# Attention with eight query heads on two key heads: the linear step of an exponential made on VectorE in place of GpSimd, groups of eight in place of ten, K placed from GpSimd's queue

## The chip, the cores and the metric

The kernel runs on one core of a Trainium2 chip. The metric is the time of one execution in microseconds of the device. Three executions of the kernel before gave 389.97, 390.28 and 391.14 us; the median is 390.28.

The core has engines that run beside one another: TensorE (PE, matmuls; PEld is its loading of weights), VectorE (DVE), ScalarE (ACT), GpSimd (POOL) and SyncE (SP), which issues DMAs. Each works through its own queue in order and waits on semaphores of others. ScalarE and GpSimd can issue DMAs too.

## The reference

Inputs are q of 8 x 8 x 1024 x 64 (batch, query heads, positions, head width), k and v of 8 x 2 x 1024 x 64, all fp32 and about 0.1 in size. Four query heads share one key head.

```python
scale = 1.0 / np.sqrt(head_dim)
for g in range(n_kv_heads):
    scores = scale * np.matmul(q_group, k_group.transpose(0, 1, 3, 2))
    scores_max = np.max(scores, axis=-1, keepdims=True)
    attn = np.exp(scores - scores_max)
    attn = attn / (np.sum(attn, axis=-1, keepdims=True) + 1e-08)
    output[:, q_start:q_end, :, :] = np.matmul(attn, v_group)
```

The kernel doesn't subtract the maximum, since the scores are small. It gets each row's sum from a column of ones beside v.

## The kernel before

**Jobs and cells.** A job is one batch, one query head and one of two sides (the even or the odd query positions, 512 of them): 128 jobs in all. Each job has eight cells, one for each 128 key positions. A cell is one score matmul (line 426), an exponential of its 128 x 512 scores, and four output matmuls (line 490) that add up in one bank for the job. There are 1024 cells.

**Two ways to the exponential.** A cell of kind A goes to ScalarE, two cells at a time: one ACTIVATE of 128 x 1024 (line 437, tile pa). A cell of kind D goes to VectorE. Line 446 (planner's name p1) turns its scores into the bits of a bf16 number, by one multiplication and addition written as uint16. That is a rough exponential. When GROUP of these cells are gathered in a tile pd, a chain of four steps corrects all of them at once: step 0 (line 462) takes the fraction bits into z; step 1 (line 468) makes y, a linear function of z, in fp16; step 2 (line 478) multiplies y by z; step 3 (line 482) adds y to pd. The steps named in POOL_STEPS run on GpSimd, the others on VectorE. Before, step 1 is on GpSimd and GROUP is 10.

**The end of a job.** VectorE takes the reciprocal of the sums (line 503) and multiplies the outputs by it (line 506); SP stores the result (line 515).

**The planner.** The order of all this is written out ahead of time by make_plan. It simulates the engines with fixed prices (QK, PV, P1, NORM, EXP, and CHAIN as a constant and a part per cell for each of the four steps) and always takes the operation that can start first, with ties by kind. Kind A takes the cells of the current job; kind D takes cells of jobs that lie LEAD ahead (fewer at the start: one job for every RAMP jobs done), at most PER_JOB of one job, while fewer than PENDING cells wait for the end of their chain and fewer than LIVE_D groups are alive. So the prices and these limits decide how many cells go each way. A plan step that is on GpSimd is taken not to occupy VectorE.

**Loads.** A head of q or k is cast to bf16 by a DMA of GpSimd's queue into scratch memory (line 299), where it waits for a recent score matmul, so that casts keep pace with the work. SP's queue then turns it with two transposing DMAs (line 311) into qT or kT. K is held zero-padded in kset: for each side the 64 rows of one half of the partitions are zero. Four DMAs for each batch and key head (place_k, line 319) copy the pieces of kT there: 60 in all, since the first is made by other means. Values are loaded by GpSimd's queue (place_v, line 332). All of these have due times counted back from the first use of their head, th: for late heads a k cast at th - 36.5, its transposes at th - 26, the placements at th - 15, the v loads at th - 12, a q cast at th - 27 and its transposes at th - 18. at_pool is at, except that it moves a due time that falls in a GpSimd chain step to the end of that step. Each queue gets its steps in order of due time.

Of the kernel before, what the change touches and what calls it, by code (L numbers as in the profile page):

```python
# [11 lines left out]

CURVE_A, CURVE_B = 0.32988085, -0.33401025

GROUP = 10
POOL_STEPS = (1,)


def make_plan(nj, nkc):
# [6 lines left out]

    QK, PV, P1, NORM = 0.216, 0.1225, 0.603, 0.555
    EXP = (0.065, 0.4265)
    CHAIN = ((0.20, 0.133), (0.25, 0.43), (0.16, 0.27), (0.16, 0.27))
    FROM_PE, FROM_ACT, FROM_DVE, FROM_POOL = 0.26, 0.17, 0.10, 0.15  # L30
    LIVE_A, LIVE_D, PENDING, PER_JOB, LEAD, RAMP, AHEAD, FIRST_PV = 28, 5, 20, 2, 8, 6, 0.08, 2.0
    INF = 1e9
    FIRST_LOAD, EACH_LOAD = 4.5, 4.2
    ops = []
# [20 lines left out]
    while normed < nj:  # L55
# [22 lines left out]
        for i, s in enumerate(open_jobs):  # L78
            for c in rem[s]:
                at = max(pe, FIRST_PV, ready.get(s * nkc + c, INF))  # L80
                if at < INF:
                    best = min(best or (INF,), (at, 3 + i, "pv", (s, c)))
        if len(open_jobs) < 2 and next_job < nj:
            at = min(ready.get(next_job * nkc + c, INF) for c in range(nkc))
            at = max(pe, FIRST_PV, min(obank_free), at)
            if at < INF:
                best = min(best or (INF,), (at, 3 + len(open_jobs), "open", next_job))
        for q, p, kind in ((normq, 0, "norm"), (p1q, 1, "p1"), (chainq, 2, "chain")):
            if q:
                at = q[0][0]  # L90
                if kind != "chain" or q[0][3] not in POOL_STEPS:
                    at = max(dve, at)
# [64 lines left out]
        elif kind == "p1":  # L157
# [8 lines left out]
            home[cell] = ("D", d_id)  # L166
            if len(cur) == GROUP:
                chainq.append((dve + FROM_DVE * (0 in POOL_STEPS), d_id, cur, 0))
                cur = []
        elif kind == "flush":  # L170
            chainq.append((dve + FROM_DVE * (0 in POOL_STEPS), d_id, cur, 0))
            cur = []
        else:
            _, g, cells, step = chainq.pop(0)
            ops.append((t, "chain", g, len(cells), step))
            end = t + CHAIN[step][0] + CHAIN[step][1] * len(cells)
            dve = end if step not in POOL_STEPS else dve
            if step + 1 < len(CHAIN):
                at = end
                if (step in POOL_STEPS) != (step + 1 in POOL_STEPS):  # L180
                    at += FROM_POOL if step in POOL_STEPS else FROM_DVE
                chainq.insert(0, (at, g, cells, step + 1))
# [9 lines left out]
def kernel(  # L192
# [7 lines left out]
    nc = tc.nc  # L200
# [30 lines left out]

    jobs = [(b, h, side) for b in range(B) for h in range(H) for side in range(2)]
    plan = make_plan(len(jobs), NKC)
    starts = {}
    for op in plan:
# [44 lines left out]
    def at(t, f, *args):  # L280
        events.append((t, len(events), f, args))

    def at_pool(t, f, *args):

        for first, last in chains:
            if first - POOL_DMA < t < last:
                t = last + 0.01
        at(t, f, *args)
# [27 lines left out]
        transpose(("k", b, g), kT[(b, g)], n)  # L316

    def place_k(b, g, side, parity):
        nc.sync.dma_start(  # L319
            out=ksets[b % 2][  # L320
                side * D : (side + 1) * D, g, side, parity * HALF : (parity + 1) * HALF
            ],
            in_=kT[(b, g)][parity * D : (parity + 1) * D, :],
        )
# [118 lines left out]
    def exp_bits(cell, n, g, slot):  # L443
        if slot == 0:
            groups[g] = pd_pool.tile([128, GROUP, QBS], U16, name="pd")
        nc.vector.tensor_scalar(  # L446
# [9 lines left out]
    def exp_curve(g, m, step):  # L456
        pd = groups[g][:, 0:m]
        eng = nc.gpsimd if step in POOL_STEPS else nc.vector
        if step == 0:
            z = tmp_pool.tile([128, GROUP, QBS], U16, name="z")[:, 0:m]  # L460
            temps[g] = [z]
# [3 lines left out]
        elif step == 1:  # L465
            y = tmp_pool.tile([128, GROUP, QBS], FP16, name="y")[:, 0:m]
            temps[g].append(y)
# [55 lines left out]
    for op in plan:  # L523
        if op[1] == "qk":
            first_use.setdefault(op[2] // (2 * NKC), op[0])
        elif op[1] == "norm":
            b, h, side = jobs[op[2]]
# [10 lines left out]
    for b in range(B):  # L538
        for h in range(H):
            if b == 0 and h == 0:  # L540
                continue
            th = first_use[b * H + h]
            spare = min(1.0, max(0.0, th - 12.0) / 60.0)
            if (b, h) not in ((0, 1), (0, 2)):
                casts.append((th - 13.0 - 14.0 * spare, ("q", b, h), q[b, h]))
            for n in range(HALF // PIECE):
                at(th - 8.0 - 10.0 * spare + n, transpose_q, b, h, n)
            if h % HPG == 0:
                g = h // HPG
                th = min(first_use[b * H + h + i] for i in range(HPG))  # L550
                casts.append((th - 16.5 - 20.0 * spare, ("k", b, g), k[b, g]))
                for n in range(HALF // PIECE):
                    at(th - 11.0 - 15.0 * spare + n, transpose_k, b, g, n)
                for side in range(2):
                    for parity in range(2):
                        at(th - 6.0 - 9.0 * spare, place_k, b, g, side, parity)
                for two in range(2):
                    at_pool(th - 4.0 - 8.0 * spare + two, place_v, b, g, two)
    casts.sort(key=lambda e: e[0])
# [43 lines left out]
```

## Time and profile before

| what | us |
|---|---|
| median of three runs | 390.28 |
| the profiled execution, whole | 391.14 |
| its span, first to last instruction | 389.4 |
| ScalarE busy | 376.5, of them 374.0 in 406 exponentials |
| TensorE busy | 362.7 |
| VectorE busy | 350.6 |
| GpSimd busy | 166.6, of them 94.6 in 22 chain steps |
| DMA, mean rate | 117 GB/s |

The granted TensorE clock is 1.000 in the whole span. Busy times are unions: an instruction that starts while the one before it drains adds only what it adds. So the mean duration of an ACTIVATE is 1060 ns, but 406 of them fill 374.0 us, 921 ns each. In a row of groups the parts are: line, engine, operation, tiles and shapes, count, then busy time and mean nanoseconds of one, then the engine's idle time before these instructions and what ended most of it.

### The profile page before, as it was taken

The numbers are of one execution on the slowest core, as the hardware profiler recorded it, in microseconds if no ns is written. First come the engines' busy times: TensorE is split into PE (matmuls) and PEld (weight loads), VectorE is DVE, ScalarE is ACT, GpSimd is POOL, SyncE is SP. The second block draws the span as 40 slices with busy tenths as digits, with TensorE's granted clock in tenths as the row PEclk, the third lists the DMA queues.
The fourth block names the chain that finished last, engine by engine and source line by source line (L and its number), as shares of the span: only waits on it lengthen the run. The fifth ranks groups of instructions, "written<-read, shape, count | busy, mean of one in ns | idle before, by whom it ended". The sixth has DMA issues, their size and how long they took to land.

```text
span 389.4 us, 12414 instructions
## 1 busy us (share of the span) xinstructions
PE 362.7 (93%) x5080; PEld 234.1 (60%) x5172; DVE 350.6 (90%) x545; ACT 376.5 (97%) x410; POOL 166.6 (43%) x147
## 2 busy tenths in 40 slices
PE   7979999989999998999999999999999999999986
PEld 5425565556566665676666656666555666665654
DVE  4789999889989999899999999999998999999782
ACT  5999999989999999999999999999999999999995
POOL 5494543437152543525254463525165352421410
PEclk9999999999999999999999999999999999999999
DMA  7768949494958676595968658493775948220213
GB/s 128 130 136 108 139 89 135 105 162 95 152 103 123 140 126 124 110 155 108 157 130 129 141 101 136 109 185 83 131 133 106 165 103 135 67 73 29 65 47 82
DMA packets 104921, 45.52 MB, mean 117 GB/s; under 512 B 66272, under 2 KB 103393, under 8 KB 103617
## 3 DMA queue, kind: packets, MB, share of 16 engines
q1 hardware_dynamic: 84592, 31.22, 34.2%
q0 software_dynamic: 19728, 13.25, 30.4%
q8 instruction: 40, 0.66, 0.7%
q10 hardware_dynamic: 544, 0.26, 0.2%
q14 instruction: 17, 0.13, 0.2%
HBM read 25.17 MB, written 27.00 MB: 134 GB/s over the span
## 4 chain that ended last, share of the span: by engine, by line
ACT 66%; PE 16%; issue 6%; DMA 5%; DVE 5%; SPq 2%; POOL 0%; POOLq 0%; ACTq 0%
ACT pa L437 66%; PE aps L426 7%; PE ops L490 6%; DMA qT<-scr_q 3%; PE dps L426 3%; DVE pd L446 2%; SPq L311 1%; DMA scr_q<-in_q_dram 1%; DMA kset<-kT 1%; DVE ost L506 1%; DVE pd L482 1%; DVE y L478 1%; SPq L319 1%; DVE z L462 0%; DVE rec L503 0%
## 5 line engine op out<-in xcount | busy, mean ns | idle before, releaser
L437 ACT ACTIVATE pa<-aps 128x1024 bf16<-128x1024 f32 x406 | 374.0, 1060 | 5.1 <-PE aps L426 4.3
L426 PE MATMUL aps<-qT,kset 128*128 128x512 bf16 x721 | 221.4, 378 | 13.0 <-ACT pa L437 11.3
L490 PEld LDWEIGHTS <-pa 128*128 128x128 bf16 x3248 | 136.7, 97 | 59.3 <-issue 0.8
L490 PE MATMUL ops<-vset,pa 128*128 128x65 bf16 x3248 | 150.2, 194 | 2.5
L446 DVE TENSOR_SCALAR pd<-dps 128x512 uint16<-128x512 f32 x212 | 138.1, 684 | 14.3 <-PE dps L426 13.4
L468 POOL TENSOR_SCALAR y<-z 128x5120 f16<-128x5120 uint16 (+1 forms) x22 | 94.6, 4300 | 89.7 <-DVE z L462 54.9
L426 PEld LDWEIGHTS <-kset 128*128 128x128 bf16 x1024 | 81.9, 97 | 65.9 <-issue 29.1
L426 PE MATMUL dps<-qT,kset 128*128 128x512 bf16 x211 | 73.4, 379 | 5.0 <-DMA qT<-scr_q 1.5
L299 POOL DMA_DIRECT2D scr_q<-in_q_dram x63 | 34.8, 553 | 89.5 <-PE aps L426 69.6
L478 DVE TENSOR_TENSOR y<-z,y 128x5120 f16<-128x5120 uint16 (+1 forms) x22 | 59.8, 2719 | 0.1
L482 DVE TENSOR_TENSOR pd<-pd,y 128x5120 uint16<-128x5120 uint16 (+1 forms) x22 | 59.8, 2720 | 0.1
L506 DVE TENSOR_TENSOR ost<-ops,rec 128x256 f32<-128x256 f32 x128 | 54.4, 425 | 4.4
L490 PEld LDWEIGHTS <-pd 128*128 128x128 bf16 x848 | 40.5, 97 | 24.7 <-DVE pd L482 2.3
L490 PE MATMUL ops<-vset,pd 128*128 128x65 bf16 x848 | 46.3, 194 | 1.0
L503 DVE RECIPROCAL rec<-ops 128x4 f32<-128x4 f32 x128 | 22.7, 177 | 13.2 <-PE ops L490 12.3
L462 DVE TENSOR_SCALAR z<-pd 128x5120 uint16<-128x5120 uint16 (+1 forms) x22 | 31.6, 1436 | 0.1
L332 POOL DMA_DIRECT2D vset<-in_v_dram x32 | 24.9, 783 | 0.0
L299 POOL DMA_DIRECT2D scr_k<-in_k_dram x15 | 7.8, 521 | 28.2 <-PE aps L426 16.0
L381 PE MATMUL ops<-blank 128*128 128x128 bf16 x40 | 4.8, 297 | 1.1 <-DVE blank L264 1.1
L381 PEld LDWEIGHTS <-blank 128*128 128x128 bf16 x40 | 4.1, 141 | 1.1 <-DVE blank L264 1.1
L339 POOL DMA_DIRECT2D kset<-kset x6 | 4.1, 694 | 0.0
L389 ACT ACT_TABLE_LOAD x1 | 1.3, 1283 | 1.8 <-issue 1.8
(20 smaller groups left out, 9.2 us busy)
## 6 DMA issues: line engine op xcount, KB each, us to landing
out_dram<-ost SPq DMA_DIRECT2D x63, 256.0 KB, 3.5
scr_q<-in_q_dram POOLq DMA_DIRECT2D x63, 128.0 KB, 3.8
kset<-kT SPq DMA_DIRECT2D x60, 64.0 KB, 3.3
vset<-in_v_dram POOLq DMA_DIRECT2D x32, 64.0 KB, 4.6
qT<-scr_q SPq DMA_TRANSPOSE x126, 3.6
scr_k<-in_k_dram POOLq DMA_DIRECT2D x15, 128.0 KB, 3.3
kset<-kset POOLq DMA_DIRECT2D x7, 128.0 KB, 3.7
kT<-scr_k SPq DMA_TRANSPOSE x30, 3.9
```

Source lines behind the costliest of these rows:

```text
L299: dma = nc.gpsimd.dma_start(out=scr.rearrange("(p f) -> p f", f=1024), in_=src.rearrange("(p s) d -> p (s d)", s=1024 // D),)
L332: nc.gpsimd.dma_start(out=vsets[b % 2][:, g, two * NHC : (two + 1) * NHC, 0:D], in_=v[b, g].rearrange("(c p two) d -> two p c d", p=128, t ...
L426: last_score[0] = nc.tensor.matmul(dst, lhsT=ksets[b % 2][:, h // HPG, side, c * 128 : (c + 1) * 128], rhs=qT[(b, h)], start=True, stop=Tr ...
L437: nc.scalar.activation(out=pt[:, 0:m], in_=psum.pop(("A", n))[:, 0:m], func=AF.Exp, scale=scale)
L446: nc.vector.tensor_scalar(out=groups[g][:, slot], in0=psum.pop(cell), scalar1=bits_scale, scalar2=bits_bias, op0=ALU.mult, op1=ALU.add,)
L462: eng.tensor_scalar(out=z, in0=pd, scalar1=0x7F, scalar2=None, op0=ALU.bitwise_and)
L468: eng.tensor_scalar(out=y, in0=temps[g][0], scalar1=CURVE_A / 128.0, scalar2=CURVE_B, op0=ALU.mult, op1=ALU.add,)
L478: eng.tensor_tensor(out=y, in0=z, in1=y, op=ALU.mult)
L482: eng.tensor_tensor(out=pd, in0=pd, in1=y, op=ALU.add)
L490: nc.tensor.matmul(ops_of[s][:, qs, :], lhsT=p_of[cell][:, qs * 128 : (qs + 1) * 128], rhs=vsets[b % 2][:, h // HPG, c, :], start=opens an ...
L503: nc.vector.reciprocal(out=rec, in_=o[:, :, D])
L506: nc.vector.tensor_tensor(out=stage[(b, h)][:, :, side, :], in0=o[:, :, 0:D], in1=rec.unsqueeze(2).to_broadcast([128, NQS, D]), op=ALU.mult,)
```

## The change

GROUP becomes 8, and POOL_STEPS is empty, so all four chain steps run on VectorE. The planner's price of step 1 becomes that of step 0. PENDING goes from 20 to 16, PER_JOB from 2 to 3, LEAD from 8 to 6. The placements of K are issued on GpSimd's queue in place of SP's, by at_pool; with no chain step on GpSimd, at_pool moves nothing.

```diff
-GROUP = 10
-POOL_STEPS = (1,)
+GROUP = 8
+POOL_STEPS = ()
@@ make_plan
-    CHAIN = ((0.20, 0.133), (0.25, 0.43), (0.16, 0.27), (0.16, 0.27))
+    CHAIN = ((0.20, 0.133), (0.20, 0.133), (0.16, 0.27), (0.16, 0.27))
     FROM_PE, FROM_ACT, FROM_DVE, FROM_POOL = 0.26, 0.17, 0.10, 0.15
-    LIVE_A, LIVE_D, PENDING, PER_JOB, LEAD, RAMP, AHEAD, FIRST_PV = 28, 5, 20, 2, 8, 6, 0.08, 2.0
+    LIVE_A, LIVE_D, PENDING, PER_JOB, LEAD, RAMP, AHEAD, FIRST_PV = 28, 5, 16, 3, 6, 6, 0.08, 2.0
@@ place_k
-        nc.sync.dma_start(
+        nc.gpsimd.dma_start(
             out=ksets[b % 2][
                 side * D : (side + 1) * D, g, side, parity * HALF : (parity + 1) * HALF
             ],
@@ the due times
                 for side in range(2):
                     for parity in range(2):
-                        at(th - 6.0 - 9.0 * spare, place_k, b, g, side, parity)
+                        at_pool(th - 6.0 - 9.0 * spare, place_k, b, g, side, parity)
```

## The prediction

> **What bounds the kernel now.** I read the page's engine totals, then its groups, then the chain that ended last, then the busy time by stage.
>
> ```profile
> span 389.4 us, 12414 instructions
> PE 362.7 (93%) x5080; PEld 234.1 (60%) x5172; DVE 350.6 (90%) x545; ACT 376.5 (97%) x410; POOL 166.6 (43%) x147
> ...
> L437 ACT ACTIVATE pa<-aps 128x1024 bf16<-128x1024 f32 x406 | 374.0, 1060 | 5.1 <-PE aps L426 4.3
> ...
> L446 DVE TENSOR_SCALAR pd<-dps 128x512 uint16<-128x512 f32 x212 | 138.1, 684 | 14.3 <-PE dps L426 13.4
> L468 POOL TENSOR_SCALAR y<-z 128x5120 f16<-128x5120 uint16 (+1 forms) x22 | 94.6, 4300 | 89.7 <-DVE z L462 54.9
> ```
>
> ScalarE has 406 exponentials of two score cells each. They fill 374.0 us without a hole worth the name: 0.921 us a pair, 0.461 us a cell. The first starts at 6.98 and the last ends at 385.1, so 4.1 us of that stretch are idle; with 7.0 before and 4.3 after, that is the span. VectorE makes the other 212 of the 1024 cells (212 rows of L446). So the time is the number of cells on ScalarE, times 0.461, and VectorE's speed decides that number. The chain agrees:
>
> ```profile
> ACT 66%; PE 16%; issue 6%; DMA 5%; DVE 5%; SPq 2%; POOL 0%; POOLq 0%; ACTq 0%
> ```
>
> The answer by stage (columns: window, PE, PEld, DVE, ACT, POOL busy, clock, DMA share, GB/s) shows whether VectorE has room:
>
> ```profile
> 7.00:17.30 10.30, 8.81 (x79) 4.43 (x79) 5.99 (x10) 9.40 (x11) 3.55 (x7) 1.00 0.70 121
> 17.30:40.00 22.70, 18.84 (x151) 9.18 (x153) 20.25 (x29) 22.70 (x25) 16.55 (x15) 1.00 0.78 126
> ...
> 280.00:340.00 60.00, 57.50 (x819) 37.14 (x831) 57.17 (x89) 59.81 (x66) 27.44 (x20) 1.00 0.67 116
> 340.00:361.70 21.70, 20.90 (x300) 13.37 (x302) 20.80 (x30) 21.60 (x24) 4.46 (x1) 1.00 0.18 50
> 361.70:386.30 24.60, 22.30 (x395) 15.79 (x399) 16.20 (x32) 23.43 (x26) 5.50 (x2) 1.00 0.24 68
> ```
>
> From 280 to 361.7 VectorE is busy 78.0 of 81.7 us. Over all stages from 7.0 to 386.3 its busy times add to 347.4 of 379.3: 31.9 us idle, of which 4.3 lie before 17.3, 8.4 after 361.7, and 19.2 (5.6%) between. Two engines are full at once; work added to one must be paid.
>
> **The chain step that comes to VectorE.** Durations from start to start of back-to-back instructions in the timeline: two L446 take 1.28 with 0.68 for one alone, so 0.60 each; L462 on 5120 elements 1.40 (89.58 to the next start at 90.98); L478 and L482 2.73 each (97.14 to 99.87); a reciprocal and its product 0.21 + 0.34 = 0.55.
>
> Before, a group of ten costs VectorE 6.0 + 1.40 + 2 x 2.73 = 12.86, or 1.286 a cell. The check: 212 x 1.286 + 128 x 0.55 = 343.0, beside 350.6 busy with the start's copies in it.
>
> After, a group has eight cells. L462 is 1484 ns at 5120 and 420 at 1024 elements, 0.266 us per 1024, so 1.13 at 4096; L478 falls from 2816 and 691 by the same slope (0.53 per 1024) to 2.20. The new step on VectorE (L468: uint16 in, fp16 out, multiply and add) is not in the trace there. Nearest low row: L462, also one two-byte tensor in SBUF to another, 1.13. Highest: L446, from fp32 scores, 8 x 0.60 = 4.8. I take 1.13, because only operation and output type differ from L462. By the Trainium skill (VectorE: DVE Perf Modes, "The perf-mode tier table") a tensor-scalar on two-byte data in SBUF gets the fourfold rate; L462's slope agrees, and no row here shows it for a fp16 result.
>
> Group of eight: 4.8 + 2 x 1.13 + 2 x 2.20 = 11.46, or 1.433 a cell: 0.147 more. With 212 cells that is 31.2 us of new VectorE work. GpSimd's 94.6 us go, but nothing on the chain is GpSimd's. L478 needs the new step's result; L478 and L482 run behind one another with 0.1 us idle, so the hand-over costs nothing, and GpSimd's wait for it (54.9 us behind L462) is gone.
>
> **How many cells move.** If VectorE's idle time stays, each cell that moves frees 1.433 there and lengthens the run by 0.461: 31.2 / 1.894 = 16.5 cells. The planner decides by its own prices (0.603 + 0.725 = 1.328 a cell before, 0.603 + 0.896 = 1.499 after, 0.459 on ScalarE): 212 x 0.171 / 1.958 = 18.5 cells. Since these prices set the order, I take 18. LEAD 6 lets the last VectorE cells lie two jobs (some 5.8 us) nearer the end, where 8.4 us idle; half of it, 4.2, gives 4.2 / 1.894 = 2 cells back. PER_JOB 3 widens the window of jobs ahead from 4 to 6 cells and PENDING 16 still allows two groups: ends 0 to 4 cells back, taken 0. Net 16 cells: 196 on VectorE, 414 exponentials, 8 x 0.921 = **+7.4 us**. TensorE does the same matmuls; at 57 busy of 60 it takes no harm from a slower pace. GROUP 8 makes some 25 groups instead of 22; their fixed costs are in the sums above.
>
> **The K placements.** 60 DMAs leave SP's queue (median 0.594 us of issue, 36 us in all) and enter GpSimd's, where the nearest row (L339, same kind) has 0.53 median: 32 us, against 94.6 freed. They land in 3.3 now; L339's in 3.7. New wait: in GpSimd's queue a placement waits for its K transposes on SP, with casts and v loads behind it. SP reaches placements late (transposes issued from 72.40 to 76.86 land by 80.8, placement at 82.68), so GpSimd will be there first and stand for up to some 7 us a set, 15 sets. Cover: a cast is due 9 planned us ahead of its transposes and lands in 3.8, so 5 us are spare, and GpSimd already stands 89.7 us before L468. Without this cover, 2 us a set at two or three sets: +2 to +6 at the worst; taken 0. SP gains: its transposes and output stores no longer queue behind placements. Two holes of ScalarE bear on this, 1.03 us at 84.87 (behind a qT transpose of 5.50) and 0.48 at 154.63 (behind a placement):
>
> ```profile
> 78.19 5.50 DMA qT<-scr_q
> ...
> 84.87 0.88 ACT pa L437
> ```
>
> I count -0.5, ends -1.5 and +2.
>
> Against this move stands a row: a cast's issue at 89.58 took 1.59 us beside L462's 1.48, where the median is 0.51.
>
> ```profile
> 89.58 1.59 POOL L299 DMA_DIRECT2D scr_q<-in_q_dram  x1 [6.12 <-PE aps L426]
> 89.58 1.48 DVE L462 TENSOR_SCALAR z<-pd 128x5120 uint16<-128x5120 uint16 x1
> ```
>
> Two such steps per group, 2 x 24.5 x 1.2 = 59 us, are 15% of the run: 9 of 60 placements caught, some 0.6 us each, 5 us of queue time, none on the path. The Trainium skill (SBUF — State Buffer, "Who interferes with whom") says that VectorE in a two-port mode locks GpSimd out of writing descriptors for the whole instruction, and advises the SP or ACT queue: against this change. Taken at its worst, every set late by 0.5 us as that at 154.63, it makes 15 x 0.5 = 7 us, 404 in place of 397; the rows give 0.
>
> **Sum.** 7.4 - 0.5 = +6.9: span 396.3, and with the 1.74 us that lie around it 398.0; the profiled run (391.14) stands 0.86 above the median of 390.28, so 397.2.
>
> **Rivals.** (1) Not slower: VectorE's idle time takes the 31.2 us and no cell moves. Then only -1.5 is left, 388.8. For it: 31.9 us are idle. Against: 12.7 of them lie at both ends; filling all 19.2 between leaves (31.2 - 19.2) / 1.894 = 6 cells, +2.9 - 1.5, 391.7. It decides where fewer than 3 cells move (1.4 us). (2) The new step runs at half L462's rate, 2.20: 1.07 x 24.5 = 26 us that the planner does not know of; its prices hold 196 x 0.066 = 13 in reserve, the rest is late, and TensorE then waits for score banks: 397.2 + 13 = 410. It begins at about 1.7 us a step. At L446's rate, 80 us more. For it: only the missing row. (3) Loads come late behind GpSimd's new waits: +2 to +6, 399 to 403. For it: the row at 89.58 and the late transposes; against: SP waited for a cast only 7.0 us in all, three times.
>
> **Numbers.** My forecast 0.74 (its own range 394.5 to 399.5: 10 to 21 cells moved), rival 1 0.09, rival 2 0.07, rival 3 0.10. The range of 393.5 to 402 leaves out rival 2, most of rival 1 and a little of rival 3. Within 0.3% (about what a measurement of this kernel can tell from no change) is 389.1 to 391.5: half of rival 1, 0.04; faster 0.05; slower 0.91.
>
> **What would show it.** L437 at x410 to x418 with 0.921 each; L446 near x196; a VectorE row for L468 near 1218 ns; L478 and L482 near 2285; ScalarE's idle at most 5; VectorE some 95% busy between 17 and 360; L319 on GpSimd's queue, waiting for kT. Wrong if L446 stays above 206, if L468 is above 1.7 us, or if ScalarE's holes exceed 7 us with DMA as their releaser.

## The result and the profile after

The changed kernel takes 392.9 us, the kernel before 390.1 beside it: 1.0068 times as long, 95% interval 1.0045 to 1.0091. It is slower, as forecast, but by 2.8 us where 6.9 were forecast, and 392.9 lies just under the range (393.5 to 402).

From the page of the changed kernel, the lines that answer to those of before:

```profile
span 390.8 us, 12423 instructions
PE 363.8 (93%) x5081; PEld 233.9 (60%) x5172; DVE 366.4 (94%) x573; ACT 380.6 (97%) x415; POOL 111.1 (28%) x185
...
ACT 74%; PE 19%; issue 5%; DMA 1%; DVE 0%
...
L437 ACT ACTIVATE pa<-aps 128x1024 bf16<-128x1024 f32 x411 | 378.2, 1068 | 2.4 <-PE aps L426 1.7
...
L446 DVE TENSOR_SCALAR pd<-dps 128x512 uint16<-128x512 f32 x202 | 130.8, 683 | 4.8 <-PE dps L426 4.2
...
L319 POOL DMA_DIRECT2D kset<-kT x60 | 34.6, 587 | 3.0 <-DMA kT<-scr_k 1.7
L468 DVE TENSOR_SCALAR y<-z 128x4096 f16<-128x4096 uint16 (+1 forms) x26 | 31.6, 1215 | 0.0
```

ScalarE still sets the time. It has 411 exponentials in place of 406; VectorE has 202 cells in place of 212. Ten cells moved, not sixteen. GpSimd's step is now a VectorE row of 31.6 us, and VectorE waits less: 4.8 us ahead of L446, where it was 14.3.

Busy times by stage of the changed kernel (columns: window, its length, busy time of PE, PEld, DVE, ACT and POOL, clock, DMA share, GB/s):

```profile
7.00:17.30 10.30, 8.94 (x76) 4.46 (x76) 8.27 (x12) 9.65 (x11) 4.45 (x8) 1.00 0.64 103
...
280.00:340.00 60.00, 56.92 (x799) 36.28 (x813) 58.17 (x92) 59.90 (x66) 19.94 (x30) 1.00 0.70 117
340.00:361.70 21.70, 20.64 (x311) 13.53 (x313) 21.16 (x35) 21.53 (x25) 0.00 (x0) 1.00 0.30 75
361.70:386.30 24.60, 23.15 (x396) 16.14 (x399) 21.09 (x35) 24.60 (x27) 0.00 (x0) 1.00 0.19 54
```

VectorE (third busy time) is fuller at both ends and in the middle: 8.27, 58.17, 21.16 and 21.09 us in these four stages, where it was 5.99, 57.17, 20.80 and 16.20. From the first exponential to the end of the last, one line of the kernel before and one of the changed kernel:

```profile
6.98:385.13 378.15, 356.71 (x5019) 228.70 (x5108) 346.77 (x532) 374.04 (x406) 162.97 (x135) 1.00 0.66 117
```

```profile
6.76:386.36 379.60, 358.07 (x5020) 228.71 (x5108) 362.65 (x560) 378.18 (x411) 107.58 (x173) 1.00 0.67 117
```

Two differences in these lines carry the rest of this text. VectorE's idle time is the window less its busy time: 378.15 - 346.77 = 31.4 us before, 379.60 - 362.65 = 16.9 after. ScalarE's holes are the same with its own column: 4.1 before, 1.4 after. The span then closes: +4.1 us of exponentials (378.18 - 374.04), -2.7 of holes, -0.2 because the first starts earlier, +0.2 behind the last one (4.4 in place of 4.3): +1.4, as 390.8 - 389.4. The medians differ by more than the spans, since the profiled execution before (391.14) was 1.0 over its median of 390.12 and the one after (392.61) 0.3 under.

### The profile page after: what moved, and what is told of

The parts are those of the page before. It is cut to its first block, busy times and chain, and to the rows that moved or that the text cites. A ratio compares the mean times of both kernels' runs of the same rounds, so it can differ in the third digit from the quotient of the medians.

```text
span 390.8 us, 12423 instructions
## 1 busy us (share of the span) xinstructions
PE 363.8 (93%) x5081; PEld 233.9 (60%) x5172; DVE 366.4 (94%) x573; ACT 380.6 (97%) x415; POOL 111.1 (28%) x185
## 3 DMA queue, kind: packets, MB, share of 16 engines
q1 hardware_dynamic: 79792, 27.29, 31.2%
## 4 chain that ended last, share of the span: by engine, by line
ACT 74%; PE 19%; issue 5%; DMA 1%; DVE 0%
ACT pa L437 74%; PE aps L426 8%; PE ops L490 6%; PE dps L426 3%; PE ops L381 1%; DMA kset<-kset 1%; DVE kset L363 0%; PE dps L354 0%; DVE ost L506 0%; DVE rec L503 0%; DVE blank L264 0%; PE dps L397 0%
## 5 line engine op out<-in xcount | busy, mean ns | idle before, releaser
L437 ACT ACTIVATE pa<-aps 128x1024 bf16<-128x1024 f32 x411 | 378.2, 1068 | 2.4 <-PE aps L426 1.7
L446 DVE TENSOR_SCALAR pd<-dps 128x512 uint16<-128x512 f32 x202 | 130.8, 683 | 4.8 <-PE dps L426 4.2
L426 PEld LDWEIGHTS <-kset 128*128 128x128 bf16 x1024 | 82.2, 97 | 70.4 <-issue 36.3
L426 PE MATMUL dps<-qT,kset 128*128 128x512 bf16 x202 | 70.0, 378 | 1.8 <-DMA kset<-kset 0.7
L482 DVE TENSOR_TENSOR pd<-pd,y 128x4096 uint16<-128x4096 uint16 (+1 forms) x26 | 57.8, 2223 | 0.3
L478 DVE TENSOR_TENSOR y<-z,y 128x4096 f16<-128x4096 uint16 (+1 forms) x26 | 57.7, 2221 | 0.1
L490 PEld LDWEIGHTS <-pd 128*128 128x128 bf16 x808 | 37.3, 97 | 21.1 <-DVE ost L506 0.5
L490 PE MATMUL ops<-vset,pd 128*128 128x65 bf16 x808 | 41.8, 193 | 0.7
L319 POOL DMA_DIRECT2D kset<-kT x60 | 34.6, 587 | 3.0 <-DMA kT<-scr_k 1.7
L468 DVE TENSOR_SCALAR y<-z 128x4096 f16<-128x4096 uint16 (+1 forms) x26 | 31.6, 1215 | 0.0
L462 DVE TENSOR_SCALAR z<-pd 128x4096 uint16<-128x4096 uint16 (+1 forms) x26 | 31.0, 1191 | 0.0
L332 POOL DMA_DIRECT2D vset<-in_v_dram x32 | 28.8, 905 | 3.0 <-issue 3.0
```

The lines of the kernel that those rows point to most:

```text
L319: nc.gpsimd.dma_start(out=ksets[b % 2][side * D : (side + 1) * D, g, side, parity * HALF : (parity + 1) * HALF], in_=kT[(b, g)][parity * D ...
L332: nc.gpsimd.dma_start(out=vsets[b % 2][:, g, two * NHC : (two + 1) * NHC, 0:D], in_=v[b, g].rearrange("(c p two) d -> two p c d", p=128, t ...
L426: last_score[0] = nc.tensor.matmul(dst, lhsT=ksets[b % 2][:, h // HPG, side, c * 128 : (c + 1) * 128], rhs=qT[(b, h)], start=True, stop=Tr ...
L437: nc.scalar.activation(out=pt[:, 0:m], in_=psum.pop(("A", n))[:, 0:m], func=AF.Exp, scale=scale)
L446: nc.vector.tensor_scalar(out=groups[g][:, slot], in0=psum.pop(cell), scalar1=bits_scale, scalar2=bits_bias, op0=ALU.mult, op1=ALU.add,)
L462: eng.tensor_scalar(out=z, in0=pd, scalar1=0x7F, scalar2=None, op0=ALU.bitwise_and)
```

## The experiments

The change is a bundle: a step that changes engine, four limits of the planner, and a queue. The theory after the result: before, VectorE's gaps were there because of the step on GpSimd. While a group is away, its cells count against PENDING and its next steps can't run. With the step on VectorE no group is away, so half of the added work found free time. Rivals: the limits closed the gaps, or the placements did.

Here are all kernels, with exponentials, ScalarE's holes and VectorE's idle time (both between first and last exponential, in the one profiled execution of each) and the ratio to the kernel before. The experiments ran in three sets, e1 to e4, e5 to e8 and e9 to e12, each with the kernel before beside it (medians 391.1, 389.9 and 389.9 us), so the ratio, and not the time, is what can be compared from one set to another:

| kernel | exponentials | holes, us | VectorE idle, us | ratio (95%) |
|---|---|---|---|---|
| before | 406 | 4.1 | 31.4 | 1 |
| e1_step | 410 | 6.8 | 21.1 | 1.0147 (1.0107 to 1.0188) |
| e7_group8 | 412 | 1.9 | 22.4 | 1.0135 (1.0092 to 1.0178) |
| e11_lead8 | 412 | 1.3 | 21.7 | 1.0085 (1.0058 to 1.0113) |
| e10_pj2 | 411 | 1.6 | 15.0 | 1.0051 (1.0023 to 1.0079) |
| e4_after_sp | 411 | 2.2 | 17.7 | 1.0076 (1.0050 to 1.0103) |
| after | 411 | 1.4 | 16.9 | 1.0068 (1.0045 to 1.0091) |
| e2_settings | 408 | 5.3 | 38.7 | 1.0104 (1.0062 to 1.0146) |
| e3_place | 406 | 3.6 | 30.9 | 0.9992 (0.9966 to 1.0017) |
| e5_half | 404 | 4.2 | 26.6 | 1.0033 (1.0002 to 1.0064) |
| e6_double | 417 | 12.5 | 77.1 | 1.0621 (1.0583 to 1.0658) |
| e8_tuned | 403 | 6.4 | 24.5 | 1.0033 (1.0014 to 1.0053) |
| e9_margin | 405 | 3.4 | 26.4 | 0.9976 (0.9946 to 1.0007) |
| e12_prices | 404 | 5.1 | 27.3 | 0.9989 (0.9951 to 1.0027) |

### The step alone

```diff
-POOL_STEPS = (1,)
+POOL_STEPS = ()
-    CHAIN = ((0.20, 0.133), (0.25, 0.43), (0.16, 0.27), (0.16, 0.27))
+    CHAIN = ((0.20, 0.133), (0.20, 0.133), (0.16, 0.27), (0.16, 0.27))
```

> The kernel before with only the linear step on VectorE (POOL_STEPS empty and its price in CHAIN), all limits (GROUP 10, PENDING 20, PER_JOB 2, LEAD 8) and the placements as before. The order that it writes out has 410 exponentials and 204 VectorE cells. Theory (VectorE's 31.9 us of idle time came from cells that wait for GpSimd's step and count against PENDING): VectorE's idle time between first and last exponential falls to 22 us or less, ScalarE's holes stay near 4 us, time 393.5 to 395. Rival (the limits filled the gaps): idle stays at 28 us or more and the time is 396 or more. My prediction's own sum (idle stays whatever is done) would have been 397.

Measured: 396.9 us, ratio 1.0147. VectorE's idle time fell to 21.1 us with every limit as before, so the step filled a third of the gaps: the theory's part. The time missed its 393.5 to 395: ScalarE's holes rose to 6.8 us in the profiled execution (7.2 in a later expectation, which counts from 7.0 us). That execution, 398.05 us, is the longest of six; three took 395.8 to 396.0. One of the holes is 3.3 us long. TensorE's waits show where it begins (columns: start, duration, instruction; in brackets TensorE's idle time and what ended it):

```profile
86.92 0.54 PE L490 MATMUL ops<-vset,pd 128*128 128x65 bf16 x12 [1.40 <-DVE pd L482]
...
89.71 1.04 PE L426 MATMUL aps<-qT,kset 128*128 128x512 bf16 x2
```

TensorE works in the order written. An output matmul of a VectorE cell stood at the head of its queue while steps 2 and 3 of a group of ten ran behind one another (2.8 us each), and the scores for ScalarE stood behind it. The order itself holds this hole. By make_plan's prices, which know no clock, ScalarE idles 3.16 us in the step-alone order, behind the same exponential, the 83rd: all 28 tiles pa that LIVE_A allows are then full and wait for output matmuls behind the late cell. In all that order plans 5.1 us of holes, where the orders of the kernels before and after plan 0.7 and 0.8.

Something else came on top: two score matmuls took 1.04 us where they take 0.59 elsewhere. The stages around this show why (the number behind POOL's count is the granted clock):

```profile
85.50:87.00 1.50, 0.10 (x4) 0.09 (x4) 1.50 (x2) 0.77 (x1) 0.51 (x1) 1.00 0.76 201
87.00:88.50 1.50, 1.27 (x26) 0.80 (x27) 1.43 (x6) 0.00 (x0) 0.00 (x0) 0.99 0.82 132
88.50:90.00 1.50, 1.28 (x14) 0.78 (x12) 1.50 (x4) 0.44 (x1) 0.00 (x0) 0.50 0.63 174
90.00:91.50 1.50, 1.50 (x13) 0.82 (x12) 1.15 (x1) 1.23 (x2) 0.00 (x0) 0.50 0.24 55
```

After a stand of 1.4 us the clock is 0.50 for some 3 us. Two small holes right behind the long one, 0.27 and 0.70 us, are not in the order; whether the slow clock also lengthened the long one can't be read off, since its 3.3 us are about what the order plans.

### The limits alone

```diff
-GROUP = 10
+GROUP = 8
-    LIVE_A, LIVE_D, PENDING, PER_JOB, LEAD, RAMP, AHEAD, FIRST_PV = 28, 5, 20, 2, 8, 6, 0.08, 2.0
+    LIVE_A, LIVE_D, PENDING, PER_JOB, LEAD, RAMP, AHEAD, FIRST_PV = 28, 5, 16, 3, 6, 6, 0.08, 2.0
```

> The kernel before with only the limits of the change (GROUP 8, PENDING 16, PER_JOB 3, LEAD 6); the linear step stays on GpSimd. The order has 408 exponentials and 208 VectorE cells. Theory (GpSimd's step makes the gaps): VectorE's idle time rises above 32 us, since groups are away on GpSimd as often and fewer cells may wait; time 392 to 394. Rival (the limits filled the gaps): idle below 25 us and time at most 391.

Measured: 1.0104 (394.5 us), idle 38.7 us: the gaps grew, and the time is 0.5 us above what was expected. The rival that the limits closed them alone falls; on top of the step they close some more (21.1 us with the step alone, 17.7 in e4_after_sp, which has the step and all limits). With the limits alone, VectorE stands for GpSimd itself: 9.7 us ahead of L478 in this run, where all its waits there are 0.1 us before.

### The placements, moved alone and moved back

```diff
-        nc.sync.dma_start(
+        nc.gpsimd.dma_start(
             out=ksets[b % 2][
...
-                        at(th - 6.0 - 9.0 * spare, place_k, b, g, side, parity)
+                        at_pool(th - 6.0 - 9.0 * spare, place_k, b, g, side, parity)
```

> The kernel before with only the placements of K moved to GpSimd's queue. Same order of the other work, 406 exponentials. If the placements are what closed ScalarE's holes (4.1 us before, 1.7 after), the holes fall below 2.5 us and the time to 388 to 389. If the holes came from casts held up by GpSimd's chain step, they stay at 3.5 us or more, and the time is 389.8 to 391.

> The changed kernel with the placements of K back on SP's queue. 411 exponentials as in the changed kernel. If the placements closed ScalarE's holes: holes 3.5 us or more, time 394.5 to 395.5. If not: holes at most 2.5 us, time 392.5 to 393.5.

Measured: moved alone 0.9992 (391.0), moved back in the changed kernel 1.0076 (393.8) against 1.0068. Neither differs from its neighbour beyond the intervals. The holes of ScalarE are 3.6 and 2.2 us: the placements are not what closed most of them (4.1 before, 1.4 after; the 1.7 in the first expectation is not what the table's count gives). The first expectation's second case held in its numbers, but no run shows its cause, casts held up by GpSimd's step. The second expectation was missed by 0.3 us on its upper side.

### Less and more of GpSimd's step

Half of the step (the linear factor is left out of the result, as the expectation says), and the step twice:

```diff
-    CHAIN = ((0.20, 0.133), (0.25, 0.43), (0.16, 0.27), (0.16, 0.27))
+    CHAIN = ((0.20, 0.133), (0.25, 0.215), (0.16, 0.27), (0.16, 0.27))
...
-                out=y,
-                in0=temps[g][0],
+                out=y[:, 0 : m // 2],
+                in0=temps[g][0][:, 0 : m // 2],
...
-            eng.tensor_tensor(out=y, in0=z, in1=y, op=ALU.mult)
+            eng.tensor_tensor(out=y, in0=z, in1=z, op=ALU.subtract)
```

```diff
-    CHAIN = ((0.20, 0.133), (0.25, 0.43), (0.16, 0.27), (0.16, 0.27))
+    CHAIN = ((0.20, 0.133), (0.50, 0.86), (0.16, 0.27), (0.16, 0.27))
...
-            eng.tensor_scalar(
+            for _ in range(2):
+                eng.tensor_scalar(
...
```

> The kernel before with GpSimd's step on half of each group's cells and its price cut to match (0.215 a cell). It leaves out the linear factor: step 2 subtracts z from itself in place of multiplying it by y, with the same shapes and types, so the correction added is zero. The order has 404 exponentials and 216 VectorE cells. Theory (the gaps are groups away on GpSimd): VectorE's idle time between the first and the last exponential falls from 31.4 to 26 us or less with VectorE's own instructions unchanged; time 388 to 389.5 where the kernel before has 390. Rival (the gaps belong to the hand-overs between TensorE and VectorE, whoever makes the linear factor): idle stays at 30 or more and the time within 0.5 us of before.

> The kernel before with GpSimd's step made twice in a row, and its price doubled. The order has 417 exponentials and 190 VectorE cells. Theory: VectorE's idle time more than doubles, 65 us or more, and the time goes to 402 to 416. Rival (the gaps don't come from GpSimd): idle at most 45, time below 398.

Idle of VectorE: 26.6 us with half the step (2.3 us a group), 31.4 with the whole (4.5), 77.1 with two (8.9), and 21.1 with none on GpSimd. It follows GpSimd's time, with the planner's price of the step moved along with it. The first value misses its bound of 26 by 0.6, but is nowhere near the rival's 30. The time of the half step did not follow: 391.0 us where 388 to 389.5 were expected, 1.0033 with two exponentials fewer. Its executions ran from 389.2 to 394.5 us, and the profiled one (389.8) has a hole of 1.5 us at 143.65; what the slower ones met is not recorded. Twice the step gave 414.2 us, as expected.

The gaps can be seen where they lie. For each group, take the stretch from the end of step 0 to the start of step 2, in which the group is away on GpSimd (after: waits for its turn on VectorE). The sums over all groups, first of the kernel before (22 groups), then of the limits alone (26), then of the changed kernel (26):

```profile
sum 120.69, PE 117.46 PEld 76.71 DVE 104.46 ACT 120.50 POOL 111.50; mean PE 5.34 PEld 3.49 DVE 4.75 ACT 5.48 POOL 5.07
```

```profile
sum 107.22, PE 104.19 PEld 71.95 DVE 82.45 ACT 105.76 POOL 99.34; mean PE 4.01 PEld 2.77 DVE 3.17 ACT 4.07 POOL 3.82
```

```profile
sum 111.18, PE 107.92 PEld 75.88 DVE 105.40 ACT 110.87 POOL 35.05; mean PE 4.15 PEld 2.92 DVE 4.05 ACT 4.26 POOL 1.35
```

Before, VectorE idles 120.69 - 104.46 = 16.2 us in these stretches, more than half of its 31.4 in a third of the time. With the limits alone it is 24.8; in the changed kernel 5.8. So 10.4 of the 14.4 us by which the idle time fell lie there.

The differences are in the order itself. By its own prices make_plan leaves VectorE idle, between the order's first and last exponential, for 21.1 us before, 8.5 with the step alone, 26.6 with the limits alone and 4.3 after the change. The measured idle times are 10 to 13 us larger in each, so the order accounts for nearly all of the differences. In it the part of the theory that names PENDING holds for the limits and not for the kernel before: with the step on GpSimd and groups of eight (PER_JOB 2, LEAD 8) the planned idle time is 29.5 us at PENDING 16 and 19.7 at 24; in the kernel before it is 21.1 at 20 and still 20.8 at 24. What else in the order leaves VectorE without a cell while a group is away was not taken apart.

### Which limit

GROUP 8 and PENDING 16 on top of the step; then the changed kernel with one limit put back each:

```diff
-GROUP = 10
-POOL_STEPS = (1,)
+GROUP = 8
+POOL_STEPS = ()
...
-    LIVE_A, LIVE_D, PENDING, PER_JOB, LEAD, RAMP, AHEAD, FIRST_PV = 28, 5, 20, 2, 8, 6, 0.08, 2.0
+    LIVE_A, LIVE_D, PENDING, PER_JOB, LEAD, RAMP, AHEAD, FIRST_PV = 28, 5, 16, 2, 8, 6, 0.08, 2.0
```

> The kernel before with the linear step on VectorE, GROUP 8 and PENDING 16; PER_JOB 2, LEAD 8 and the placements as before. 412 exponentials, 200 VectorE cells. With the step alone (groups of ten) ScalarE had 7.2 us of holes and 396.9 us. If the length of a group's chain made those holes (TensorE's queue stands behind a cell whose chain is late), they fall to 3 us or less and the time to 393.5 to 395. If PER_JOB 3 and LEAD 6 are what mends it, the holes stay at 6 us or more and the time at 397 or more.

```diff
-    LIVE_A, LIVE_D, PENDING, PER_JOB, LEAD, RAMP, AHEAD, FIRST_PV = 28, 5, 16, 3, 6, 6, 0.08, 2.0
+    LIVE_A, LIVE_D, PENDING, PER_JOB, LEAD, RAMP, AHEAD, FIRST_PV = 28, 5, 16, 2, 6, 6, 0.08, 2.0
```

> The changed kernel with PER_JOB 2 in place of 3. 411 exponentials, 202 VectorE cells, as in the changed kernel. With GROUP 8 and PENDING 16 alone the time was 1.0135 of before, with LEAD 6, PER_JOB 3 and the placements as well 1.0068. If LEAD 6 brings that gain: 392.5 to 393.7. If PER_JOB 3 brings it: 394.2 or more.

```diff
-    LIVE_A, LIVE_D, PENDING, PER_JOB, LEAD, RAMP, AHEAD, FIRST_PV = 28, 5, 16, 3, 6, 6, 0.08, 2.0
+    LIVE_A, LIVE_D, PENDING, PER_JOB, LEAD, RAMP, AHEAD, FIRST_PV = 28, 5, 16, 3, 8, 6, 0.08, 2.0
```

> The changed kernel with LEAD 8 in place of 6. 412 exponentials, 200 VectorE cells. If LEAD 6 brings the gain: 394.2 or more, with VectorE idle 21 us or more between first and last exponential. If PER_JOB 3 brings it: 392.5 to 393.7.

With GROUP 8 and PENDING 16 ScalarE's holes are 1.9 us in place of 6.8, although two more exponentials are needed; the order says the same (0.9 planned in place of 5.1), and the clock stays at 1.00 until the last exponentials. The times don't tell the two kernels apart: 394.6 and 396.9 us are from different sets, the intervals of 1.0135 and 1.0147 overlap, two of the six executions took 399.1 and 399.9, and the profiled one (393.8) is the shortest of its six, where that of the step alone is the longest. The numbers of its expectation held, but not its cause, a shorter chain (steps of 2.28 us and not 2.82): GROUP and PENDING were not run apart, and in the order PENDING 16 alone, with groups of ten, leaves 0.6 us of holes, GROUP 8 alone 2.7. LEAD 6 brings 0.7 us more: with LEAD 8 the changed kernel takes 394.0 us (393.4 to 394.6 in all executions), with LEAD 6 and PER_JOB 2 it takes 393.3 (392.7 to 393.4). That is two cells, 0.92 us of exponentials, as VectorE's last cells lie later: the last L446 starts at 368.5 us and not at 363.0, and VectorE's idle time is 15.0 us and not 21.7. (The two differ in PER_JOB as well, which changes the count of neither.) PER_JOB 3 brings nothing that can be seen. LEAD 8's 394.0 is 0.2 under its bound, its idle time of 21.7 within.

### Tries for a faster kernel

All keep the step on GpSimd. The first has PENDING 18, PER_JOB 3, LEAD 7; the second adds the margin; the third has prices nearer to the rows:

```diff
-    LIVE_A, LIVE_D, PENDING, PER_JOB, LEAD, RAMP, AHEAD, FIRST_PV = 28, 5, 20, 2, 8, 6, 0.08, 2.0
+    LIVE_A, LIVE_D, PENDING, PER_JOB, LEAD, RAMP, AHEAD, FIRST_PV = 28, 5, 18, 3, 7, 6, 0.08, 2.0
```

> The kernel before with PENDING 18, PER_JOB 3 and LEAD 7, step and placements as before; a try for a version faster than both. 403 exponentials, 218 VectorE cells. If VectorE's gaps close as the order says and ScalarE's holes stay near 4 us: idle 25 us or less, time 387.5 to 389. If three cells of one job in a row make TensorE wait for score banks: holes 6 us or more, time 390 or more.

```diff
-    FROM_PE, FROM_ACT, FROM_DVE, FROM_POOL = 0.26, 0.17, 0.10, 0.15
+    FROM_PE, FROM_ACT, FROM_DVE, FROM_POOL = 0.26, 0.17, 0.10, 0.80
```

> As the try with PENDING 18, PER_JOB 3 and LEAD 7, but the planner allows 0.80 us in place of 0.15 for the hand-over from GpSimd back to VectorE. 405 exponentials, 214 VectorE cells. That try had 403 exponentials, 6.4 us of holes in ScalarE and no gain. If its holes came from hand-overs that were later than planned (TensorE then stands, and its clock falls to half), they shrink to 4 us or less and the time is 388 to 390. If the holes have another cause: 6 us or more and 391 or more.

```diff
-    CHAIN = ((0.20, 0.133), (0.25, 0.43), (0.16, 0.27), (0.16, 0.27))
-    FROM_PE, FROM_ACT, FROM_DVE, FROM_POOL = 0.26, 0.17, 0.10, 0.15
-    LIVE_A, LIVE_D, PENDING, PER_JOB, LEAD, RAMP, AHEAD, FIRST_PV = 28, 5, 20, 2, 8, 6, 0.08, 2.0
+    CHAIN = ((0.10, 0.133), (0.25, 0.43), (0.06, 0.27), (0.06, 0.27))
+    FROM_PE, FROM_ACT, FROM_DVE, FROM_POOL = 0.26, 0.17, 0.10, 0.50
+    LIVE_A, LIVE_D, PENDING, PER_JOB, LEAD, RAMP, AHEAD, FIRST_PV = 28, 5, 18, 2, 7, 6, 0.08, 2.0
```

> The kernel before with the planner's prices of VectorE's chain steps near what the trace shows (constants 0.10 and 0.06 in place of 0.20 and 0.16), 0.50 us for the hand-over from GpSimd, PENDING 18 and LEAD 7; a second try for a version faster than both. 404 exponentials, 216 VectorE cells. If the order can be kept: idle of VectorE 26 us or less, ScalarE's holes at most 4, time 387.5 to 389.3. If the hand-overs come late: holes 6 us or more, time 390 or more.

The first has three exponentials fewer than before (2.8 us) and is no faster (1.0033): its holes are 6.4 us. The numbers are those of the second case of its expectation, but the largest hole, 1.92 us, is no wait for score banks. It is not in the order either; a late hand-over is the cause. Step 2 (L478) waited 1.46 us for GpSimd, the normalisation came behind it, and TensorE stood for that; the stages of this kernel show the clock again:

```profile
278.98 2.83 DVE L478 TENSOR_TENSOR y<-z,y 128x5120 f16<-128x5120 uint16 x1 [1.46 <-POOL y L468]
...
282.41 0.65 PE L490 MATMUL ops<-vset,pa 128*128 128x65 bf16 x16 [1.59 <-DVE ost L506]
```

```profile
280.80:282.40 1.60, 0.02 (x1) 0.00 (x0) 1.56 (x4) 1.21 (x2) 0.66 (x1) 1.00 0.98 145
282.40:284.00 1.60, 1.59 (x19) 0.89 (x19) 1.56 (x3) 0.06 (x1) 0.00 (x0) 0.69 1.60 153
284.00:286.00 2.00, 2.00 (x16) 1.11 (x15) 2.00 (x2) 1.32 (x2) 0.52 (x1) 0.50 0.68 161
```

What made GpSimd late here is its own queue. Step 0 had ended at 272.49, but step 1 began at 274.47, behind a cast that had waited 8.15 us for a score matmul. With 0.80 us for the hand-over the holes fall to 3.4 us, as expected (the largest, 1.99, stands where the order plans 1.66), and the median is 389.5 us: ratio 0.9976, interval 0.9946 to 1.0007. That is the best kernel here and clearly ahead of the changed one, but ahead of the kernel before by no more than can be told from nothing. The prices nearer to the rows gave 0.9989: two levels of time, 388.6 to 388.9 and 390.9 to 393.8, neither hand-overs kept nor always lost. Its expectation held in neither form.

## Why the prediction was wrong

**What bounds the kernel: right.** ScalarE's exponentials at 0.921 us a pair carry the time; ScalarE is busy 0.92 us a pair in every kernel of the table. What the table adds is that its holes range from 1.3 to 12.5 us.

**The new step's price: right.** 1.13 us on VectorE was taken from step 0's row; the changed kernel has 150.22 to 151.35 from start to start, 1217 ns in the median. Step 2 was put at 2285 ns and is 2281. The rival with half the rate falls. VectorE's added work follows: 202 x 1.433 + 70.4 = 359.9 against 343.0 before is 16.9; its busy time between first and last exponential rose by 15.9.

**"If VectorE's idle time stays": the step that failed.** It gave 16.5 cells, and the planner's prices gave 18.5 by the same assumption. The idle time fell from 31.4 to 16.9 us. Put into the same formula, (31.2 - 14.4) / 1.894 = 8.9 cells; ten moved, two cells given back by LEAD included. That makes +4.1 us of exponentials in place of +7.4. The fall for LEAD was forecast, at 4.2 us; the fall of 10.3 that the step alone brings was put at nothing. The count needed no estimate: make_plan, run with the new constants, writes 411 exponentials, where the sum had 414. The trace of before had the sign: 5.5 us passed on average between step 0 and step 2 of a group, and 16.2 of the 31.4 idle us lay there. I read GpSimd as free because nothing on the chain was GpSimd's, and wrote that "the hand-over costs nothing" because L478 hardly waited. But the chain names what ended last, and the cost of the hand-over was in the order written out ahead: fewer VectorE cells than VectorE had time for. None of the three signs of being wrong that the prediction named came.

**Rival 1 (idle time takes the work)** stood at 0.09, and for the case that only the gaps in the middle fill it had 391.7. The truth, 392.9, is between that and the forecast. The split was made as if the gaps either stay or go.

**LEAD, PER_JOB, PENDING.** Two cells for LEAD 6: right, to the cell (202 with 6, 200 with 8). PER_JOB 0: right. GROUP 8 was costed only at its fixed parts, and PENDING 16 at nothing. With the step on VectorE the two remove holes of ScalarE (6.8 to 1.9 us in the profiled executions, 5.1 to 0.9 in the order); that was missed, and what it is worth in time is not shown (1.0147 and 1.0135).

**ScalarE's holes**: -0.5 was taken, with -1.5 as the end; it is -2.7. The two at 69.91 and 84.87, and the one at 154.63, are gone. With the placements alone moved these three are gone as well, but others, of 1.63 us at 31.46 and 0.43 at 33.83, stand in their place (3.6 in all, time unchanged); with the placements moved back in the changed kernel they don't return. So the sum of the holes isn't the placements' doing. Nor is it the order's, which plans 0.7 us before and 0.8 after. What took the 2.7 us away stays open; it is the second term that was mis-sized.

**The placements: right.** 0 on the path. GpSimd's wait for the K transposes, put at up to 7 us a set, was 1.7 us in all. The Trainium skill (SBUF — State Buffer, "Who interferes with whom") advises against this queue beside VectorE's fast steps. The rows agree in kind: five of the sixty placement issues took 1.15 to 1.30 us where the median is 0.52, and during each of the five an L462 or L468 began on VectorE. At fifteen planned us ahead it costs nothing that can be measured here (0.9992, 0.9966 to 1.0017).

## What to carry to other kernels

Where an order is written out ahead with prices and limits, idle time of a full engine is not a constant: ask which limit or hand-over makes it before you price work added there, and price the case that it goes as its own. If you hold the program that writes the order, run it: it gives the count and the planned gaps before anything runs on the chip. Moving a step to the fuller engine costs less than its duration if the hand-over kept that engine waiting. And limits belong to the kernel they were chosen for: with their placements left on SP, the same limits made the version without hand-over 3 us better (396.9 to 393.8) and the one with it 3 to 4 us worse.

## What was not expected of the hardware

TensorE's granted clock fell to about 0.5 for some 3 us after stands of 1.40 us (the step alone), 1.59 (the first try), 1.67 (the placements alone, at 30) and 2.08 (the step twice), each in the middle of dense work. It did not after stands of 1.34 (an earlier one in the step twice), 1.50 (the limits alone), 1.55 (the half step) and 1.68 us (the third try). The kernel before and the changed kernel have no such dip before the last exponential. The Trainium skill (TensorE: Matmul & The Clock Gate, "Part 1: The HAM clock gate (the "warmup" mystery)") speaks of an idle window of about 3.4 us that runs freely; here less than half of it was enough (1.40 to 1.67 us, three times), and not each time. That it depends on where a stand falls in such a window was not shown.

Executions of one kernel lie up to several us apart, with the hand-over (5.1 us in the third try) and without it (6.2 with GROUP 8 and PENDING 16 on top of the step). In the first try the mean granted clock goes with the time: 0.993 to 0.994 in the five executions of 391.9 to 392.3 us, 0.998 to 0.999 in the seven of 389.8 to 390.6, as a dip in some of them would make it. It is not the only cause: the two longest of the half step, 394.4 and 394.5 us, have 1.000 and 0.999.
